# One compare for both one-hot tiles, their gates multiplied on ScalarE, and a norm's inverse root through logarithm and exponential

## The chip, the cores and the metric

The kernel runs on one core of one Trainium2 chip. The metric is the device time of one execution in microseconds. Three runs of the kernel before took 4728.34, 4738.8 and 4741.7 us; the median is 4738.8 us.

Five engines work side by side, each taking its own instructions strictly in order, and wait for one another by semaphores: TensorE (PE in the rows, with PEld for its weight loads) multiplies matrices, VectorE (DVE) and ScalarE (ACT) work on tiles element by element, GpSimd (POOL) does the same more slowly and issues the row gathers, SyncE (SP) issues most transfers. TensorE runs at one of two clock levels, 1.2 or 2.4 GHz; the profile gives the granted clock of a stretch as a share of the higher one.

## The reference

One inference step of a decoder with two layers, over 512 prompt tokens and 8 x 8 sample tokens, all in float32. In each layer one projection feeds three mixers (attention over a window, gated linear attention called GLA, pooling). Their results are gated, added, projected, and a layer norm follows; then comes a layer of 16384 one-neuron experts ("PEER"), and another layer norm. Two pieces matter here.

The GLA mixer ends in a norm per head:

```python
ob = ob * lax.rsqrt(jnp.mean(jnp.square(ob), -1, keepdims=True) + RMS_EPS) * gla_norm_g.astype(jnp.float32)
ob = (ob.astype(x.dtype) * jax.nn.silu(gb.reshape(Bx, T, B_HEADS, B_DV))).reshape(Bx, T, B_V)
```

The expert layer picks, for each token and each of 8 heads, 16 of 128 x 128 experts, and weighs them by a softmax:

```python
eidx = jnp.take_along_axis(cidx.reshape(...), ci, axis=-1)
g = jax.nn.softmax(cscore, axis=-1)
h = jax.nn.gelu(jnp.einsum('thkd,td->thk', u, xi, ...), approximate=False)
return jnp.einsum('thk,thkd->td', (g * h).astype(v.dtype), v)
```

So each token has 128 picked experts (8 heads x 16), each with a gate `g`.

## The kernel before

**Stages of a layer.** The tokens are cut into two groups. Group 0 (256 prompt tokens and the 64 sample tokens, 320 columns) goes through the mixers first (`_p1`: attention, the branch of it, GLA, GLA's norm and branch, pooling and its branch, the output projection and layer norm); then its expert scores are made (`_query`). Group 1 (256 prompt tokens) goes through the same `_p1` with a background: while it runs, the experts of group 0 are selected. Then group 1's scores are made, and the dense stage follows: all 128 rows of experts are multiplied for 384 tokens, while the remaining 192 tokens fetch their experts row by row (`uvr`, gathered by GpSimd and weighed on VectorE). In the trace the first layer's group 0 takes about 0 to 560 us and its scores to 700 us, group 1's mixers to 1160 us, its scores to 1250 us, the dense stage to 2400 us; the second layer repeats this from there on.

**The scatter of the gates (`_spread`, L941 to L972).** The dense stage needs, for each expert and token, the gate or zero. `_spread` makes it for four tokens at a time. A tile `oh` holds two one-hot tables for them: `oh[:, 1]`, with a row for each of a token's 128 picks and a one in the column of one half of the expert's number (one compare of 128 x 512 on VectorE, L951), and `oh[:, 0]`, the same for the other half, with the gate in place of the one. For that the count `n.act_mul` says how many of the four tokens are compared without a gate (L953) and multiplied by it on ScalarE (L958); the others take one VectorE instruction each that compares and multiplies (L960). TensorE multiplies the two tables of each token (L964), ScalarE copies the product into a staging tile `gst` (L965), and four transfers take each 32 tokens to memory (L971). Group 0's 256 tokens make 64 such fours in each layer, in the background of group 1's mixers, with `act_mul` 0; the last 128 tokens make 32 fours ahead of the dense stage, with `act_mul` 2 (L1171).

**The norm (`_phase_gla_out`, L567 to L601).** For each of four heads, GpSimd squares the two halves of the GLA output `oT`, TensorE sums them over the partitions with a matrix of ones (`ps_ssq`, L578), VectorE scales and adds the epsilon (L580), ScalarE takes the root in place (L583), and VectorE the reciprocal in place (L584). Each of the eight `oT` is then multiplied by that (L594) and by the gate of `gb` (L599). This is done four times: for each group of each layer, on 320 or 256 columns.

**The order.** Nobody writes the engines' order out. A scheduler places the instructions by priority and by its own reckoning of when each could start; the order on each engine is fixed when the program is built. The background of group 1's mixers is handed to it piece by piece, one or more at each fetch of a weight block (`tick`, L157), with a lower priority (`LAGB`). Weight blocks are cut on arrival into two parts for TensorE: ScalarE casts the high part (`whi`, L131), VectorE subtracts for the low part (`wlo`, L128), each with three buffers.

Of the kernel before, what the change touches and what calls it, by code (L numbers as in the profile page):

```python
# [15 lines left out]
AF = mybir.ActivationFunctionType  # L16
OP = mybir.AluOpType
# [549 lines left out]
def _phase_gla_out(n, l, oT):  # L567
    tc, nc, c, W = n.tc, n.nc, n.c, n.G.W
    ob = n.parts("ob")
    with tc.tile_pool(name="go_u", bufs=10) as up:  # L570
        n.up = up
        rs = []
        for h in range(4):
            ps = n.pmm.tile([128, 512], F32, tag="mm", name="ps_ssq", bufs=3)
            for dv in range(2):
                sq = n.unit("sq")
                nc.gpsimd.tensor_tensor(sq, oT[2 * h + dv], oT[2 * h + dv], op=OP.mult)
                nc.tensor.matmul(ps[:, 0:W], c["ones"], sq, start=(dv == 0), stop=(dv == 1))  # L578
            r = n.unit("rs")
            nc.vector.tensor_scalar(r, ps[:, 0:W], 1.0 / 256, RMS_EPS, op0=OP.mult, op1=OP.add)  # L580
            rs.append(r)
        for h in range(4):
            nc.scalar.activation(rs[h], rs[h], AF.Sqrt)  # L583
            nc.vector.reciprocal(rs[h], rs[h])  # L584
        for m in range(8):
            ps = n.mm(n.w_get(l, ("gb", m)), n.xs, W)
            b = BPOS["gb", m]
            th = n.unit("th")
            nc.scalar.activation(th, ps, AF.Tanh, scale=0.5, bias=n.hb[:, b:b + 1])
            xg = n.unit("xg")  # L590
            nc.scalar.activation(xg, ps, AF.Identity, bias=n.lc[:, b:b + 1])
            nc.vector.scalar_tensor_tensor(th, th, 1.0, xg, op0=OP.add, op1=OP.mult)
            o = oT[m]
            nc.vector.scalar_tensor_tensor(o, o, n.hg[:, m:m + 1], rs[m // 2], op0=OP.mult, op1=OP.mult)  # L594
            dst = [t[m // 4][:, m % 4, :] for t in ob]
            if len(dst) == 1:
                nc.vector.tensor_tensor(dst[0], o, th, op=OP.mult)
            else:
                nc.vector.tensor_tensor(o, o, th, op=OP.mult)  # L599
                n.put(dst, o)  # L600
    return [n.ks(t) for t in ob]  # L601
# [242 lines left out]
def _sel_tiles(sp, nt):  # L844
    return sp.tile([128, nt, 16, 16], F32, name="sv"), sp.tile([128, nt, 16, 16], U32, name="siu")
# [95 lines left out]
def _spread(n, gp, t, sT, new_ps, gt0=None):  # L941

    nc, c = n.nc, n.c
    iota = lambda w: c["iota"][:, None, None, :].to_broadcast([128, w, 4, 128])
    for g in range(128 // GT):
        st = gp.tile([128, 128, GT], F32, name="gst", bufs=n.gst)
        for t4 in range(0, GT, 4):
            tt = g * GT + t4
            oh = gp.tile([128, 2, 4, 128], F32, name="oh", bufs=n.job)
            w = n.act_mul  # L950
            nc.vector.tensor_tensor(oh[:, 1], iota(1)[:, 0], sT[:, 1, tt:tt + 4, None].to_broadcast([128, 4, 128]), op=OP.is_equal)  # L951
            if w:
                nc.vector.tensor_tensor(oh[:, 0, 0:w], iota(1)[:, 0, 0:w], sT[:, 0, tt:tt + w, None].to_broadcast([128, w, 128]),  # L953
                                        op=OP.is_equal)
            for k in range(4):
# [89 lines left out]
def tile_hybrid_step(ctx, tc, I, O, L):  # L1045
    nc = tc.nc
    n = Net(ctx, tc, I, O, L)
# [57 lines left out]
    for l in range(L):  # L1105
# [12 lines left out]
        gat.load(1, gpool)  # L1118
        sac, sa = scope(f"selA{l}")
        sv, siu = _sel_tiles(sa, 3)  # L1120
        n.job, n.gst, n.act_mul = 2, 1, 0
        _query(n, l, sa, [n.ks(xa[0]), n.ks(xa[1])], G0.tok, G0.W, sv, siu, n.new_mm)
        xac.close()
        sT = [sa.tile([128, 3, 128], F32, name=f"selT{t}") for t in range(2)]
# [40 lines left out]
        for q in range(2):  # L1165
            nc.gpsimd.tensor_tensor(x1W[q][:, :, 0:HB], x1A[0][q][:, :, 0:HB].bitcast(F32), x1A[1][q][:, :, 0:HB].bitcast(F32),
                                    op=OP.add)
# [40 lines left out]
        with tc.tile_pool(name=f"dense{l}", bufs=1) as dp:  # L1208
            gt, late = None, []
            for i in range(NE):  # L1210
# [12 lines left out]
                h = hs[i]  # L1223
# [206 lines left out]
```

## Time and profile before

| | |
|---|---|
| median of three runs | 4738.8 us |
| the profiled execution | 4736.97 us |
| its span, first to last instruction | 4735.2 us |
| mean granted clock of TensorE over the span | 0.978 |
| TensorE busy | 4530.7 us, 96% |
| VectorE busy | 3793.4 us, 80% |
| ScalarE busy | 1820.2 us, 38% |
| GpSimd busy | 1370.1 us, 29% |

A busy share over the whole span mixes stages with different limits, so the stage around the change has to be looked at by itself. Durations in the rows overlap a little where instructions follow each other without a wait: what one costs its engine in a row of equal ones is the step from start to start. A wait is given with the instruction that ended it.

### The profile page before, as it was taken

To read this page: it belongs to the slowest core of one execution; us is meant where nothing else is said; L and a number is where in the kernel's file an instruction comes from. 1 tells how busy PE (TensorE), PEld (TensorE's weight loads), DVE (VectorE), ACT (ScalarE), POOL (GpSimd) and SP (SyncE) were. 2 spreads that over 40 slices of the span, in tenths; PEclk is the share of its full clock that TensorE was granted. 3 is DMA by queue.
4 is the path that set the end of the run, shared out by engine and by line. 5 is a ranking of instruction groups with operands and counts; after the bars stand their busy time and mean duration, and the time that the engine had idled before them with its cause. 6 is when DMAs were issued, how large, how long until landed. Compare 5 with 4: busy or idle time off the path is not lost. (4 is left out here: it accounts for less than half of the span.)

```text
span 4735.2 us, 69451 instructions
## 1 busy us (share of the span) xinstructions
PE 4530.7 (96%) x25588; PEld 4001.3 (85%) x25588; DVE 3793.4 (80%) x7435; ACT 1820.2 (38%) x3386; POOL 1370.1 (29%) x884
## 2 busy tenths in 40 slices
PE   7999999989999999999999999999999999999998
PEld 6879977788778999999878789777887789999997
DVE  5455698697879999999964556977978799999998
ACT  3434323354343433333344343234433433333333
POOL 0011001121035555555300110011210365555552
PEclk9999999999999999999999999999999999999999
DMA  4334535566379899999723345265663798898996
GB/s 147 110 125 139 180 94 213 193 232 229 126 274 345 328 337 325 330 324 331 279 85 121 122 149 167 88 222 195 232 231 131 289 353 323 328 330 322 335 323 233
DMA packets 359521, 1093.59 MB, mean 231 GB/s; under 512 B 28495, under 2 KB 164175, under 8 KB 309709
## 3 DMA queue, kind: packets, MB, share of 16 engines
q1 hardware_dynamic: 272112, 608.88, 38.0%
q0 software_dynamic: 55296, 402.68, 22.6%
q10 hardware_dynamic: 31772, 77.60, 4.4%
q8 instruction: 201, 3.29, 0.3%
q14 instruction: 140, 1.14, 0.1%
HBM read 1014.01 MB, written 77.52 MB: 231 GB/s over the span
## 5 line engine op out<-in xcount | busy, mean ns | idle before, releaser
L128 POOL TENSOR_TENSOR wlo<-raw,whi 128x1024 fp32r<-128x1024 f32 x232 | 704.1, 3035 | 928.4 <-ACT whi L131 894.1
L131 ACT CAST whi<-raw 128x1024 fp32r<-128x1024 f32 x582 | 607.9, 1048 | 601.0 <-PE ps_mm L183 379.0
L183 PE MATMUL ps_h<-x1A,whi 128*128 128x384 f32 x3712 | 696.4, 340 | 13.3 <-ACT h L1182 13.2
L183 PEld LDWEIGHTS ps_h<-x1A,whi 128*128 128x128 f32 x3712 | 655.9, 190 | 33.6 <-ACT h L1182 17.1
L128 DVE TENSOR_TENSOR wlo<-raw,whi 128x1024 fp32r<-128x1024 f32 x350 | 432.8, 1241 | 275.2 <-ACT whi L131 136.8
L1024 DVE SCALAR_TENSOR_TENSOR zB<-uvr,hc,zB 128x1024 f32<-128x1024 f32 x380 | 587.2, 1545 | 4.7
L1006 POOL DMA_INDIRECT uvr<-uv,gidx x384 | 441.8, 1151 | 474.9 <-DVE zB L1024 209.0
L1017 DVE SCALAR_TENSOR_TENSOR uvr<-uvr,x1B 128x1024 f32<-128x1024 f32 x384 | 493.4, 1285 | 68.9 <-DMA uvr<-uv,gidx 68.6
L1236 PE MATMUL y<-vh,wh 128*128 128x512 f32 x1536 | 478.1, 393 | 0.6 <-ACT vh L131 0.6
L1236 PE MATMUL y<-vl,wh 128*128 128x512 f32 x1536 | 476.5, 391 | 0.0
L1236 PE MATMUL y<-vh,wl 128*128 128x512 f32 x1536 | 474.9, 390 | 0.3 <-DVE wl L128 0.3
L183 PE MATMUL ps_mm<-xa,whi 128*128 128x320 f32 x2400 | 413.3, 321 | 14.7 <-ACT xa L131 14.7
L1225 DVE TENSOR_TENSOR h<-h,gt 128x384 f32<-128x384 f32 x256 | 395.8, 1551 | 11.5 <-ACT h L1182 7.0
L183 PEld LDWEIGHTS ps_mm<-xa,whi 128*128 128x128 f32 x2400 | 370.7, 194 | 33.8 <-ACT xa L131 15.3
L183 PE MATMUL ps_h<-x1A,wlo 128*128 128x384 f32 x1856 | 362.7, 338 | 0.0
L1236 PEld LDWEIGHTS y<-vl,wh 128*128 128x128 f32 x1536 | 288.7, 188 | 64.2 <-DVE vl L128 0.2
L1236 PEld LDWEIGHTS y<-vh,wl 128*128 128x128 f32 x1536 | 288.7, 188 | 63.5 <-DVE wl L128 0.7
L131 ACT CAST wh<-h 128x384 fp32r<-128x384 f32 x256 | 130.5, 511 | 533.3 <-PE y L1236 502.0
L183 PEld LDWEIGHTS ps_h<-x1A,wlo 128*128 128x128 f32 x1856 | 327.1, 189 | 0.0
L1236 PEld LDWEIGHTS y<-vh,wh 128*128 128x128 f32 x1536 | 287.3, 189 | 45.7 <-ACT vh L131 1.4
L1019 ACT ACTIVATE hc<-hc 128x1 f32<-128x1 f32 x384 | 77.7, 203 | 628.1 <-DVE uvr L1017 620.3
L128 DVE TENSOR_TENSOR vl<-vr,vh 128x1024 fp32r<-128x1024 f32 x256 | 311.5, 1217 | 0.7 <-ACT vh L131 0.7
(349 smaller groups left out, 7650.3 us busy)
## 6 DMA issues: line engine op xcount, KB each, us to landing
raw<-wall SPq DMA_DIRECT2D x468, 512.0 KB
raw<-ut SPq DMA_DIRECT2D x256, 512.0 KB
vr<-vt SPq DMA_DIRECT2D x256, 512.0 KB
gd<-gst ACTq DMA_DIRECT2D x96, 512.0 KB
gt<-gd SPq DMA_DIRECT2D x62, 768.0 KB
S<-state_gla SPq DMA_DIRECT2D x8, 1024.0 KB
s_gla<-S ACTq DMA_DIRECT2D x8, 1024.0 KB
uvr<-uv,gidx POOLq DMA_INDIRECT x384
```

What stands on the lines that cost most here:

```text
L128: return eng.tensor_tensor(lo, src, hi.bitcast(F32), op=OP.subtract)
L131: return self.nc.scalar.copy(hi, src), self.sub_lo(lo, src, hi, eng)
L183: self.nc.tensor.matmul(ps[:, 0:W], w[wi][:, k * 128:(k + 1) * 128], xs[xi][k], start=(a == 0 and k == 0), stop=(a == len(pa) - 1 and k == ...
L1006: self.n.nc.gpsimd.indirect_dma_start(out=r, out_offset=None, in_=self.n.I["uv"], in_offset=bass.IndirectOffsetOnAxis(ap=self.idx[t][:, s: ...
L1017: nc.vector.scalar_tensor_tensor(r[:, 0:1024], r[:, 0:1024], 1.0, self.x[t], op0=OP.mult, op1=OP.mult, accum_out=hc[:, 0:1])
L1019: nc.scalar.activation(hc[:, 1:2], hc[:, 0:1], AF.Gelu)
L1024: nc.vector.scalar_tensor_tensor(acc, r[:, 1024:2048], hc[:, 1:2], acc, op0=OP.mult, op1=OP.add)
L1225: nc.vector.tensor_tensor(h3, h3, gt[:, :, i % 4, :], op=OP.mult)
L1236: nc.tensor.matmul(y[t][d], wt[:, ts], vt[:, d * 512:(d + 1) * 512], start=(j == 0 and a == 0), stop=(j == NE - 1 and a == 2))
```

## The change

The two compares of a four become one over both tables (1024 columns) where `act_mul` is 4, and `act_mul` becomes 4 for group 0's tokens; the gates of all four are then multiplied on ScalarE. The last 128 tokens (`act_mul` 2) take the same instructions as before. In the norm, the root and the reciprocal become a logarithm and an exponential of -0.5 times it, both on ScalarE, all four heads' logarithms written ahead of the exponentials.

```diff
         for h in range(4):
-            nc.scalar.activation(rs[h], rs[h], AF.Sqrt)
-            nc.vector.reciprocal(rs[h], rs[h])
+            nc.scalar.activation(rs[h], rs[h], AF.Ln)
+        for h in range(4):
+            nc.scalar.activation(rs[h], rs[h], AF.Exp, scale=-0.5)
...
             w = n.act_mul
-            nc.vector.tensor_tensor(oh[:, 1], iota(1)[:, 0], sT[:, 1, tt:tt + 4, None].to_broadcast([128, 4, 128]), op=OP.is_equal)
-            if w:
+            if w == 4:
+                nc.vector.tensor_tensor(oh, iota(2), sT[:, 0:2, tt:tt + 4, None].to_broadcast([128, 2, 4, 128]), op=OP.is_equal)
+            else:
+                nc.vector.tensor_tensor(oh[:, 1], iota(1)[:, 0], sT[:, 1, tt:tt + 4, None].to_broadcast([128, 4, 128]),
+                                        op=OP.is_equal)
                 nc.vector.tensor_tensor(oh[:, 0, 0:w], iota(1)[:, 0, 0:w], sT[:, 0, tt:tt + w, None].to_broadcast([128, w, 128]),
                                         op=OP.is_equal)
...
-        n.job, n.gst, n.act_mul = 2, 1, 0
+        n.job, n.gst, n.act_mul = 2, 1, 4
```

The scheduler then writes another order. In the program of the change VectorE has 128 compares of 128x1024 in place of 128 of 128x512 and 512 TENSOR_SCALAR, and 16 reciprocals fewer; ScalarE has 512 more multiplies by a gate, 16 more activations of `rs`, and 78 loads of an activation table where there were 74. The same instructions stand on TensorE, GpSimd and SyncE, some of them in another place. Lines after L583 have moved by one, those after L955 by four.

VectorE in group 1's pooling of the first layer (`u_ext`, `s_ext` and `d` belong to the pooling, `wlo` to the weights, `oh` to the scatter), before:

```order
L659 TENSOR_TENSOR s_ext<-u_ext 128x270
L951 TENSOR_TENSOR oh<-ct,selT_6264 128x512
L662 SCALAR_TENSOR_TENSOR d<-s_ext,u_ext 128x256
L960 TENSOR_SCALAR oh<-ct,selT_6264 128x128 x3
L128 TENSOR_TENSOR d_9369<-d,d_9368 128x256
L960 TENSOR_SCALAR oh<-ct,selT_6264 128x128
L128 TENSOR_TENSOR wlo<-raw,whi 128x1024
```

The same engine and place in the program of the change:

```order
L660 TENSOR_TENSOR s_ext<-u_ext 128x270
L953 TENSOR_TENSOR oh<-ct,selT_6264 128x1024
L663 SCALAR_TENSOR_TENSOR d<-s_ext,u_ext 128x256
L128 TENSOR_TENSOR wlo<-raw,whi 128x1024
L128 TENSOR_TENSOR d_9369<-d,d_9368 128x256
```

The four TENSOR_SCALAR are gone, and the weight's low part now stands ahead of that of `d`. ScalarE at this place, before:

```order
L131 CAST d_9368<-d 128x256
L131 CAST whi<-raw 128x1024
L652 ACTIVATE u_ext<-ps_mm,lc 128x256
L965 COPY gst<-ps_hr 128x128x4
L675 COPY oprow<-pt 15x128
```

and in the change:

```order
L131 CAST d_9368<-d 128x256
L653 ACTIVATE u_ext<-ps_mm,lc 128x256
L962 ACTIVATE oh<-oh,selT_6264 128x128
L969 COPY gst<-ps_hr 128x128x4
L676 COPY oprow<-pt 15x128
L962 ACTIVATE oh<-oh,selT_6264 128x128 x3
L131 CAST whi<-raw 128x1024
```

Multiplies by a gate now stand between the cast of one weight block and that of the next.

VectorE in group 0's last GLA head of the first layer, where the norm of the heads before it is already under way (`S` is the GLA state of that head, `klm` a masked key, `oT` the GLA output, `rs` the norm), before:

```order
L580 TENSOR_SCALAR rs<-ps_ssq 128x320
L506 TENSOR_TENSOR klm<-kl,ct 64x1024
L526 COPY S<-ps_S 128x256
L584 RECIPROCAL rs<-rs 128x320
L528 SCALAR_TENSOR_TENSOR S<-S,dec,ps_S 128x256
L584 RECIPROCAL rs<-rs 128x320
L528 SCALAR_TENSOR_TENSOR S<-S,dec,ps_S 128x256
L594 SCALAR_TENSOR_TENSOR oT_1732<-oT_1732,hg,rs 128x320
L528 SCALAR_TENSOR_TENSOR car_S_91<-S,dec,ps_S 128x256
```

The same place in the change:

```order
L580 TENSOR_SCALAR rs<-ps_ssq 128x320
L526 COPY S<-ps_S 128x256
L506 TENSOR_TENSOR klm<-kl,ct 64x1024
L528 SCALAR_TENSOR_TENSOR S<-S,dec,ps_S 128x256
L595 SCALAR_TENSOR_TENSOR oT_1732<-oT_1732,hg,rs 128x320
L528 SCALAR_TENSOR_TENSOR S<-S,dec,ps_S 128x256
L595 SCALAR_TENSOR_TENSOR oT_1733<-oT_1733,hg,rs 128x320
L528 SCALAR_TENSOR_TENSOR car_S_91<-S,dec,ps_S 128x256
```

The two reciprocals between the state's updates are gone, and two multiplies of `oT` stand there. ScalarE a little before, at the first head's norm, in the change (`os` is the sample tokens' GLA output, which TensorE takes next):

```order
L583 ACT_TABLE_LOAD
L583 ACTIVATE rs<-rs 128x320
L585 ACT_TABLE_LOAD
L585 ACTIVATE rs<-rs 128x320
L540 COPY os<-ps_os 64x256
```

Before, the third and fourth of these rows were not there: the copy of `os` followed the root of L583 at once.

## Rows read from the trace of the kernel before

**Rows 1.** The page's busy times: engine, us, share of the span, instructions

```profile
PE 4530.7 (96%) x25588; PEld 4001.3 (85%) x25588; DVE 3793.4 (80%) x7435; ACT 1820.2 (38%) x3386; POOL 1370.1 (29%) x884
```

**Rows 2.** Busy us of each engine in stretches, then granted clock, DMA share, GB/s

```profile
300.00:340.00 40.00, 36.77 (x174) 25.80 (x173) 25.67 (x42) 9.04 (x19) 6.35 (x8) 0.91 0.31 104
800.00:1160.00 360.00, 335.75 (x2377) 309.37 (x2375) 289.02 (x604) 164.51 (x288) 56.64 (x53) 0.97 0.58 204
1025.00:1150.00 125.00, 119.41 (x982) 117.01 (x982) 111.97 (x249) 64.35 (x109) 13.48 (x15) 0.99 0.57 192
1400.00:2325.00 925.00, 922.62 (x4663) 838.61 (x4662) 872.27 (x989) 357.74 (x609) 509.67 (x265) 1.00 0.91 331
2655.00:2700.00 45.00, 40.98 (x201) 29.72 (x200) 27.95 (x45) 10.34 (x21) 6.64 (x9) 0.92 0.37 123
3140.00:3515.00 375.00, 352.52 (x2459) 323.92 (x2457) 303.95 (x630) 166.53 (x293) 56.65 (x54) 0.97 0.59 207
```

**Rows 3.** TensorE's waits, 800 to 1160: ended by, us, times, longest

```profile
PE ps_hr L964 <- DVE oh L960: 6.1, 4, 3.9
...
PE ps_mm L183 <- DVE oc L633: 3.0, 1, 3.0
```

**Rows 4.** TensorE's waits, 3140 to 3515

```profile
PE ps_hr L964 <- DVE oh L960: 6.3, 5, 3.9
```

**Rows 5.** VectorE in order of time, 1050 to 1076: start, us, what

```profile
1055.32 1.11 DVE L960 TENSOR_SCALAR oh<-ct,selT 128x128 f32<-128x128 f32 x4
1056.35 0.69 DVE L951 TENSOR_TENSOR oh<-ct,selT 128x512 f32<-128x512 f32 x1
1056.95 1.11 DVE L960 TENSOR_SCALAR oh<-ct,selT 128x128 f32<-128x128 f32 x4
...
1072.69 2.36 DVE L128 TENSOR_TENSOR wlo<-raw,whi 128x1024 fp32r<-128x1024 f32 x2
```

**Rows 6.** ScalarE in order of time, 1255 to 1300

```profile
1281.81 1.28 ACT L958 ACTIVATE oh<-oh,selT 128x128 f32<-128x128 f32 x4 [2.65 <-DVE cv L812]
```

**Rows 7.** TensorE's waits over the span

```profile
PE ps_yr L964 <- ACT oh L958: 13.2, 12, 2.4
```

**Rows 8.** ScalarE's groups by form: xcount | busy us, mean ns | idle before

```profile
L449 ACT ACT_TABLE_LOAD x4 | 5.1, 1283 | 0.1
...
L583 ACT ACTIVATE rs<-rs 128x320 f32<-128x320 f32 x8 | 3.8, 471 | 11.3 <-DVE rs L580 11.3
```

**Rows 9.** All engines in order of time, 296 to 332

```profile
304.60 3.67 PE L538 MATMUL ps_os<-S,qm 128*64 128x256 f32 x16
...
309.56 0.43 PE L553 MATMUL ps_o<-ct,os 64*128 64x64 f32 x2 [0.24 <-ACT os L540]
...
320.36 2.13 DVE L584 RECIPROCAL rs<-rs 128x320 f32<-128x320 f32 x1
...
320.49 0.70 PE L523 MATMUL ps_S<-vb,kl 64*128 64x256 f32 x2 [0.75 <-DVE S L526]
...
322.72 2.13 DVE L584 RECIPROCAL rs<-rs 128x320 f32<-128x320 f32 x1
...
322.85 1.22 PE L523 MATMUL ps_S<-vb,kl 64*128 64x256 f32 x2 [1.30 <-DVE S L528]
...
325.63 5.29 PE L538 MATMUL ps_os<-S,qm 128*64 128x256 f32 x16 [0.95 <-DVE oT L594]
```

**Rows 10.** All engines in order of time, 926 to 962

```profile
934.48 2.08 PE L183 MATMUL ps_mm<-x,whi 128*128 128x256 f32 x16
...
958.25 0.77 PE L964 MATMUL ps_hr<-oh 128*128 128x128 f32 x2 [3.90 <-DVE oh L960]
...
958.66 2.91 PE L183 MATMUL ps_mm<-x,whi 128*128 128x256 f32 x12
```

**Rows 11.** Waits of all engines, 1000 to 1100

```profile
ACT whi L131 <- PE ps_mm L183: 21.3, 14, 3.3
```

**Rows 12.** VectorE's compares of L951 in 1025 to 1150: us, count

```profile
1025.00:1150.00 125.00, 22.31 (x30) 0.99 0.57 192
```

## The prediction

> **What bounds the kernel now.** I read the page's busy times first, then the stretches, then TensorE's waits in the stretches that the change touches, and last the order in time around the largest of those waits.
>
> The page has TensorE busy for 96% of the span, VectorE for 80% and ScalarE for 38% [rows 1]. The stretches say where these shares come from [rows 2]. In the dense stage (1400 to 2325 us, and the like of it in the second layer) TensorE is busy for 922.62 of 925 us at full clock: nothing that the change does reaches it, since that stage holds none of the changed instructions. The scatter of group 0's gates lies in group 1's mixers, 800 to 1160 us and 3140 to 3515 us. There TensorE is busy for 335.75 of 360 and 352.52 of 375 us, so that 24.2 and 22.5 us are left in which it does nothing; VectorE is busy for 289 and 304 us, ScalarE for 165 and 167. The norm of group 0 lies in 300 to 340 us, with 3.2 us of TensorE idle and a granted clock of 0.91. So the kernel is bound by TensorE, and all that the change can win is what TensorE now idles in these stretches, some 47 us in the scatter's two and 3 to 4 us in each of group 0's norms, and what it loses by a lower clock after idling. VectorE's own saving is worth only as much of it as it ends a wait of TensorE.
>
> Which waits are those? Of the scatter's two stretches, TensorE waited 6.1 and 6.3 us for the gated one-hots of L960, and twice 3.0 us for the pooling's output `oc`, which VectorE makes behind scatter work [rows 3, 4] (the row for `oc` reads the same in the second layer and stands once): 18.4 us in all. The rest of the idle time is made of smaller waits for VectorE, ScalarE and GpSimd.
>
> **The scatter: what VectorE saves.** Two fours in a row show the cost of one: from the four TENSOR_SCALAR at 1055.32 over the compare at 1056.35 to the next four at 1056.95 are 1.63 us [rows 5]. The compare of 128x1024 is not in the trace. Nearest is another float32 TENSOR_TENSOR of 128x1024, the low part of the weights: two of them take 2.36 us, so 1.18 each [rows 5]. From below, a compare of half the size takes 0.69 us [rows 5]; from above, two such take 1.38. I take 1.18. A four then costs VectorE 0.45 us less (0.94 to 0.25 by the bounds), and 128 fours 58 us, 29 in each layer (120 to 32 by the bounds). VectorE in 800 to 1160 falls from 289 to about 253 us, the norm's 7 us there included (below), 70% of the stretch in place of 80%.
>
> How much of that TensorE gets: the 18.4 us of waits above stand where VectorE has hardly a gap (1050 to 1075 us is mostly a row of instructions back to back, of which [rows 5] show some). With a quarter less scatter work in front of them I take three quarters of these waits as gone: -14 us. It may be none (the wait is then ended by something else a moment later) or all of it and some of the small ones, -25.
>
> After a long wait TensorE is also slower for a while: behind the wait of 3.90 us at 958.25, 12 matmuls took 2.91 us, where 16 of the same took 2.08 at 934.48, or 1.56 for 12 [rows 10]: 1.35 us more. There are four waits of 3.0 us or more among those of [rows 3, 4], two in each layer (3.9 and 3.0). If all go, 4 x 1.35, -5 us; if none, 0.
>
> **The scatter: what ScalarE pays.** Four multiplies by a gate in a row take it 1.28 us [rows 6]; 64 fours are 82 us in each layer. It had 165 of 360 us in work and will have about 247, 69%. Where fours stand densest, 1025 to 1150 us with 30 compares [rows 12], it goes from 64.35 to 103 of 125 us, 82% [rows 2]. It has room for this, but it stands on TensorE's path twice: the high part of every weight block is its cast, and a four's product now can't start before it has multiplied. Those are new waits. The nearest row is the last scatter (32 fours in each layer, two gates of four on ScalarE): TensorE waited 13.2 us for these multiplies over its 64 fours, 0.21 us each [rows 7]. By that the 128 fours of the first scatter would cost 26 us. But there the fours stand one behind the other, with little else for TensorE, while here they are spread among weight blocks of 3 us, with two buffers of `oh`. I take a fifth, +5 us, with 0 and 26 as ends. What lies behind a multiply that waits for its compare is, by the order shown, the cast of the next weight block; there are three buffers for these, so a delay of one four is covered, of two or three not.
>
> **The norm.** VectorE loses 16 reciprocals, 2.13 us each at 320 columns [rows 9]. In group 0 two of them stand between the updates of the GLA state, and TensorE waits for these: 0.75, 1.30 and 0.95 us at 320.49, 322.85 and 325.63 [rows 9]; the matmuls of `ps_os` behind the last then take 5.29 us, where the same sixteen took 3.67 at 304.60: 1.6 more. Sum 4.6 us in each layer. Against it stand a table load and an exponential ahead of the copy of `os`, which TensorE waited for at 309.56 [rows 9]: a load takes 1.28 us, an activation of `rs` 0.47 [rows 8], so +1.75. Net -2.9 in each layer, -6 us for both. If the state's updates wait for something else at once, only the +1.75 is left, +3.5; if the copy is not in time's way, -9. In group 1 the four reciprocals (about 1.7 us each) stand in VectorE's backlog ahead of the 3.90 us wait of [rows 10], and their going is part of the term above; the loads there fall into ScalarE's wait for the sums. If that cover is gone, the two loads and the exponentials ahead of the first gate of `gb` cost some 3 us in each layer, which three buffers of `ps_mm` take up.
>
> Each logarithm and exponential here comes with a load of its own in the program of the change, as the order shows, and the trace of before has it alike: the GLA gate's logarithm (L449) follows its exponential (L447) at once, and yet has loads of its own, 4 of 1283 ns [rows 8]. The Trainium skill (ScalarE: Activation LUTs, Table sets: the hidden batching unit) says that one set holds both, so that a logarithm and then an exponential need a single load. The trace does not agree for this program. By that rule the `os` copy would come 1.28 us earlier in each layer, and the sum would be 2.6 us lower.
>
> **The sum.** -14 (waits for VectorE) - 5 (clock) + 5 (waits for ScalarE) - 6 (norm) = -20 us. The profiled execution took 4736.97 us (span 4735.2 and 1.8 around it), so 4717 us. Its time stands 1.8 us below the median of the three runs, 4738.8, which differ by 13 us among themselves; I leave the forecast at 4717.
>
> **The rivals.**
>
> *The waits change hands.* VectorE is lighter, but TensorE then waits for ScalarE at the same places, because the four's chain (compare, multiply, product, copy) has become longer by 1.28 - 0.45 us. For it: ScalarE already spent 21.3 us of 1000 to 1100 us waiting for TensorE to free weight buffers [rows 11], in which nothing behind it moves. Against it: most of the order on TensorE stays, with the fours spread widely. The terms of the scatter then cancel (-14 - 5 + 19), only the norm is left: 4731 us.
>
> *ScalarE becomes late: slower.* Its place is the pooling and branch stretch of 1025 to 1150 us, where it would be at 82%, and in order. A multiply that waits for VectorE's compare holds the cast of the next weight block, that one TensorE; TensorE idles and drops to the lower clock, and the next four comes later still. At the last scatter's 0.21 us for each of 128 fours, and the waits for VectorE left as they are, it comes out at +26 - 6 = +20; at twice that, as four gates are on ScalarE here where two are there, at +53 - 6 = +47. I put it at 4757 us, the first of these. It decides from a cost of about 0.2 us a four, if VectorE's relief is worth nothing. The Trainium skill speaks for this one (ScalarE: Activation LUTs, Rules for kernel authors): multiplications belong on VectorE, not on ScalarE. The rows agree that a multiply is dearer there, as one four's gates take 1.28 us where VectorE compares and multiplies in 1.11.
>
> *More goes than the named waits.* The scheduler lays the lighter queue out closer, and half of the 47 us of idle time goes with the clock's losses after it: -24 - 11 (half of the 3% of clock that is missing in these 735 us [rows 2]) - 6 + 4 for new waits = -37, about 4700 us.
>
> **How the numbers follow.** 0.3% of this time, about what a measurement can tell from none, is 14 us; the bounds are 4725 and 4753. Chances: forecast 0.46 (its own range 4705 to 4728), more goes 0.13, the waits change hands 0.28, ScalarE late 0.13. Faster by over 0.3%: most of the first (0.40), all of the second, a little of the third: 0.55. Slower: 0.08 of the last. Within: 0.37. The range that leaves out no more than two in ten goes from 4696 to 4748: the lower end takes in the last rival, the upper end goes half of the way from no change to the slower one.
>
> **What would show it.** In 800 to 1160 us (or where these stages then lie) VectorE should be busy some 36 us less and ScalarE some 85 more; the waits of TensorE for `oh` from VectorE and for `oc` should be gone or under 2 us, and those for `oh` from ScalarE near 5 us over both layers. The compare should take 1.1 to 1.25 us. In group 0's norm the two stalls of 0.75 and 1.30 us should be gone, `ps_os` should take 3.7 us, and one of about 2 us for `os` should stand earlier. The dense stage should keep its length. The forecast is wrong if TensorE's idle time in the scatter's stretches is not smaller by 10 us or more; it is wrong the other way if casts of weights come late behind multiplies, with waits of TensorE on `wlo` or `whi`.

## The result, and the profile after

The changed kernel takes 4778.7 us (median of four runs, 4776.5 to 4785.3) where the kernel before takes 4737.8 beside it: ratio 1.0087, 95% interval 1.0074 to 1.0100, so 41 us slower. I had forecast 4717 us, and 4748 as the upper end. The profiled execution has a span of 4783.3 us, 48.1 more than that of before.

First the page's busy times of the changed kernel, which answer to [rows 1].

```profile
PE 4551.5 (95%) x25588; PEld 4012.3 (84%) x25588; DVE 3699.1 (77%) x6907; ACT 1983.9 (41%) x3918; POOL 1371.7 (29%) x884
```

VectorE is relieved by 94 us and ScalarE loaded with 164, as the change says. But TensorE, with the same 25588 matmuls, is busy 20.8 us longer (the mean granted clock is 0.975, before 0.978), and idle for 231.8 in place of 204.5 us (span less busy), 27.3 more. The two make up the 48.1.

Then the same stretches as in [rows 2]. The stages have shifted by up to 50 us, so these rows answer to those of before only roughly; group 1's pooling, before at 1025 to 1150, now lies at 1047 to 1172.

```profile
300.00:340.00 40.00, 35.42 (x140) 24.59 (x141) 17.01 (x32) 12.89 (x21) 4.84 (x6) 0.75 0.32 106
800.00:1160.00 360.00, 329.47 (x2245) 299.51 (x2246) 244.60 (x338) 224.54 (x526) 61.05 (x53) 0.96 0.57 196
1047.00:1172.00 125.00, 116.88 (x951) 113.91 (x951) 95.94 (x124) 94.86 (x224) 12.56 (x13) 0.99 0.56 189
3140.00:3515.00 375.00, 337.85 (x2183) 300.06 (x2182) 254.62 (x415) 215.94 (x506) 59.37 (x61) 0.95 0.57 200
```

VectorE fell to 245 us of 360 (I had said 253), yet TensorE's idle time rose from 24.2 to 30.5 us there, and from 22.5 to 37.2 in the second layer. Group 0's norm ran at a granted clock of 0.75, before at 0.91.

For a sum by stage I took, in each trace, the ends of the last matmuls of `ps_lr` (after attention), `ps_ssq` (after GLA and norm) and `ps_wo` (after the output). Lengths in us, one profile each, so a single difference of a few us says little. Group 0's GLA and norm are the exception, since many kernels below share them: with the norm of before they read 140.5 to 147.7 (22 readings, median 141.9), with the changed norm 145.5 to 148.7 (12 readings, median 148.2).

```
                        before  changed  norm alone  scatter alone
group 0 GLA+norm, 1st    142.0    148.2       148.0          144.7
group 0 GLA+norm, 2nd    141.9    145.5       148.7          147.7
group 1 to ps_lr, 1st    244.5    245.7       246.9          249.5
group 1 GLA+norm, 1st    122.8    128.8       123.3          126.0
group 1 to ps_wo, 1st    229.2    232.6       225.4          228.6
group 1 to ps_lr, 2nd    243.2    248.1       243.9          244.2
group 1 GLA+norm, 2nd    122.9    132.6       117.1          131.2
group 1 to ps_wo, 2nd    226.7    235.5       226.3          226.6
```

What TensorE waited for over the span of the changed kernel (us, times, longest):

```profile
PE ps_hr L968 <- ACT oh L962: 25.8, 25, 3.1
...
PE ps_mm L183 <- DVE th L240: 16.5, 2, 8.3
...
PE ps_os L538 <- DMA S<-state_gla: 5.6, 3, 3.0
...
PE ps_mm L183 <- DVE oc L634: 4.8, 6, 1.4
...
PE ps_o L553 <- ACT os L540: 3.8, 2, 2.0
```

The waits for `oh` from VectorE of [rows 3, 4] are gone, those for `oc` smaller. In their place stand four others. My sum had those for `oh` from ScalarE, at a fifth of this, and for `os`, at about this length (3.5 us); those for `th` and for the state it did not have. Three places show how they come about.

**Group 0's norm.** The changed kernel in order of time; behind the table loads stands the copy of `os`:

```profile
309.69 1.28 ACT L583 ACT_TABLE_LOAD   x1
...
311.48 1.28 ACT L585 ACT_TABLE_LOAD   x1
...
313.15 0.35 ACT L540 COPY os<-ps_os 64x256 f32<-64x256 f32 x1
...
313.55 0.69 PE L553 MATMUL ps_o<-ct,os 64*128 64x64 f32 x2 [2.02 <-ACT os L540]
...
319.70 3.72 PE L560 MATMUL ps_S<-vb,klm 64*128 64x256 f32 x8
...
325.52 0.38 ACTq L564 DMA_DIRECT2D s_gla<-S  x1
...
330.03 0.38 SPq L472 DMA_DIRECT2D S<-state_gla  x1
...
335.31 6.11 PE L538 MATMUL ps_os<-S,qm 128*64 128x256 f32 x16 [2.36 <-DMA S<-state_gla]
```

And three rows of the kernel before that my prediction had not read:

```profile
312.93 1.94 PE L560 MATMUL ps_S<-vb,klm 64*128 64x256 f32 x8
...
315.81 0.38 ACTq L564 DMA_DIRECT2D s_gla<-S  x1
...
320.33 0.38 SPq L472 DMA_DIRECT2D S<-state_gla  x1
```

The copy came 1.8 us later against its matmuls, as worked out. But TensorE, idle for 2.02 us, then ran at the lower of its two levels (eight matmuls 3.72 us for 1.94; 1.2 GHz for 2.4), so the state's updates ended late, its store was issued at 325.52 for 315.81, and the next state's load, which waits for the store since `S0` has one buffer, at 330.03 for 320.33. In the kernel before `ps_os` began at 325.63 [rows 9], 5.3 us after that load was issued; here 335.31, again 5.3 us after. So the load was due when the reciprocals' stalls ended; a kernel below (e5) shows it without them.

**The end of group 1's GLA.** TensorE runs out of weight blocks and waits for a gate's multiply, which stands behind a table load and two exponentials of GLA:

```profile
920.62 1.28 ACT L481 ACT_TABLE_LOAD   x1
...
923.01 0.40 ACT L962 ACTIVATE oh<-oh,selT 128x128 f32<-128x128 f32 x1
...
923.46 1.40 PE L968 MATMUL ps_hr<-oh 128*128 128x128 f32 x4 [2.47 <-ACT oh L962]
```

Behind both places TensorE is slow for longer than the wait: the granted clock of the changed kernel (third number from the end) is 0.55 and 0.72 in these stretches; in before it is 0.87 and 0.92 where they answer to (311 to 326, 901 to 931).

```profile
313.00:328.00 15.00, 14.45 (x44) 10.67 (x45) 5.46 (x13) 3.74 (x8) 1.44 (x2) 0.55 0.11 36
920.00:950.00 30.00, 24.68 (x106) 19.44 (x105) 18.20 (x21) 17.47 (x39) 12.02 (x11) 0.72 0.26 91
```

**Group 1's branches.** VectorE's row stands still at a gathered row that has not landed. Behind it is `th`, where VectorE takes a product out of PSUM (L240) and so frees the buffer that TensorE waits for. In the trace by engine:

```profile
1004.90 1.70 POOL L1010 DMA_INDIRECT uvr<-uv,gidx  x1 [6.45 <-DVE zB L1028]
...
1014.42 1.22 DVE L1021 SCALAR_TENSOR_TENSOR uvr<-uvr,x1B 128x1024 f32<-128x1024 f32 x1 [6.33 <-DMA uvr<-uv,gidx]
...
1015.57 0.41 DVE L240 SCALAR_TENSOR_TENSOR th<-th,ps_mm 128x256 f32<-128x256 f32 x1
...
1016.04 3.72 PE L183 MATMUL ps_mm<-x,whi 128*128 128x256 f32 x16 [8.27 <-DVE th L240]
```

The waits for `oh` from ScalarE lie in more than one place. Of 11.8 us in the first layer 4.1 are in GLA and up to the norm's first load, 3.1 just behind the norm's loads, 4.6 in the pooling stretch. The longest in each layer (2.70 and 3.15 us) has a transfer behind it: ScalarE's multiplies stand behind copies into `gst`, its one staging buffer, whose last transfer has not ended.

```profile
1150.34 1.07 ACT L969 COPY gst<-ps_hr 128x512 f32<-128x512 f32 x2 [2.04 <-DMA gd<-gst]
...
1151.77 1.67 PE L968 MATMUL ps_hr<-oh 128*128 128x128 f32 x8 [2.70 <-ACT oh L962]
```

### The profile page after: what moved, and what is told of

Read it like the earlier page. It is cut to its first block, busy times and chain, and to the rows that moved or that the text cites. A ratio compares the mean times of both kernels' runs of the same rounds, so it can differ in the third digit from the quotient of the medians.

```text
span 4783.3 us, 69483 instructions
## 1 busy us (share of the span) xinstructions
PE 4551.5 (95%) x25588; PEld 4012.3 (84%) x25588; DVE 3699.1 (77%) x6907; ACT 1983.9 (41%) x3918; POOL 1371.7 (29%) x884
## 3 DMA queue, kind: packets, MB, share of 16 engines
q0 software_dynamic: 55296, 402.68, 22.5%
## 4 chain that ended last, share of the span: by engine, by line
PE 79%; DVE 7%; DMA 6%; ACT 3%; issue 3%; POOL 1%; ACTq 0%; SPq 0%; DVEq 0%; POOLq 0%
PE ps_mm L183 21%; PE ps_h L183 20%; PE y L1240 20%; PE ps_yr L183 2%; PE ps_v L464 2%; PE ps_wo L755 2%; PE ps_hr L968 2%; DMA uvr<-uv,gidx 2%; DMA gd<-gst 2%; DMA raw<-wall 1%; PE ps_o L553 1%; PE po L357 1%; PE ps_sc L826 1%; PE ps_S L560 1%; PE ps_S L523 1%
## 5 line engine op out<-in xcount | busy, mean ns | idle before, releaser
L1021 DVE SCALAR_TENSOR_TENSOR uvr<-uvr,x1B 128x1024 f32<-128x1024 f32 x384 | 484.6, 1263 | 85.0 <-DMA uvr<-uv,gidx 84.3
```

What stands on the lines that cost most here:

```text
L1021: nc.vector.scalar_tensor_tensor(r[:, 0:1024], r[:, 0:1024], 1.0, self.x[t], op0=OP.mult, op1=OP.mult, accum_out=hc[:, 0:1])
```

## The experiments

Medians are given with the ratio to the kernel before that ran beside; that kernel's own medians were 4739.0 (e1 to e4), 4738.5 (e5 to e8), 4739.9 (e9 to e12), 4735.7 (e13 to e16), 4744.8 (e17) and 4732.8 (e18). Where two versions did not run side by side, a difference of their medians is uncertain by some of this spread.

**The two parts alone.** `e1_norm_only` is before with the lines of Ln and Exp; `e2_onehot_only` is the change with Sqrt and reciprocal put back.

> The norm's logarithm and exponential alone, with the scatter as it was. Theory (a late copy): in group 0's norm the copy of os comes some 1.8 us later, TensorE waits 2 us for it and runs at the lower clock for some 12 us behind, so that the last update of the GLA state, its store and the load of the next state come late; TensorE then waits for that load. In the trace of the changed kernel the stretch lost 7.5 us in the first layer and 3.6 in the second: this kernel takes about 11 us more than before, 4745 to 4753. Rival (my forecast's step): the reciprocals' going is worth more than the late copy, -6 us, 4731. Second rival: the norm is lost in the scatter's effects, no change (within 4 us).

Measured 4753.1, ratio 1.0032 [1.0016, 1.0047]: +14, at the upper end of the theory's range.

> The merged compare with the gates multiplied on ScalarE alone, with the root and the reciprocal as they were. Theory: the remaining 30 of the 41 us come from here, TensorE's waits for the gated one-hots from ScalarE (26 us in the changed kernel) and for a gather that VectorE's row waits for (8 us in each layer): 4763 to 4773. Rival: the scatter is worth little by itself and the two parts harm each other (ScalarE late because of both): 4740 to 4750, and the two parts alone add to less than half of 41 us.

Measured 4761.4, ratio 1.0039 [1.0021, 1.0056] (median +22): just under the range given, and far over the rival's. The two together make 36 of the 41 us. The table by stage shows the norm losing 6 to 7 us in each layer in group 0, and winning some 6 in all in group 1.

**Gates on VectorE, on GpSimd, on ScalarE by half.**

```
e3  + nc.vector.tensor_tensor(oh[:, 0], oh[:, 0], <gates of the four>, op=OP.mult)
e9  + nc.gpsimd.tensor_tensor(oh[:, 0], oh[:, 0], <gates of the four>, op=OP.mult)
e11   before, with act_mul = 2
```

> As the one before, but the four gates are multiplied on VectorE, in one instruction of 128x512 behind the merged compare; ScalarE has no part in the one-hots. A four costs VectorE 1.2 + 0.7 = 1.9 us, 0.3 more than before. Theory (the chain through ScalarE costs): the waits for oh from ScalarE are gone, those for oh from VectorE are as before or somewhat longer, 4736 to 4752. Rival (any change of the order costs as much, the merge itself included): 4760 or more.

4752.2, ratio 1.0031 [1.0014, 1.0049]: at the upper end of the theory's range, with 18.0 us of waits for `oh` from VectorE. It reads 9 us less than e2, but the two intervals overlap. And its GLA and norm in group 1 took 135.2 and 133.5 us, longer than e2's 126.0 and 131.2: a loss there needs no multiply on ScalarE.

> The merged compare with the old norm, and the gates multiplied on GpSimd, in one instruction of 128x512 for a four. GpSimd was busy for 29% of the span. Theory (what costs is that a four's product comes late behind a third, in-order engine, whichever it is): TensorE waits for oh from GpSimd instead, 15 us or more in all, 4750 or more. Rival (it is ScalarE's own queue, its table loads and casts, that makes the multiply late): with a nearly idle engine the waits for oh fall under 8 us in all, and the time goes to that of before or below, 4715 to 4740.

4814.4, ratio 1.0154 [1.0137, 1.0171]. The waits on GpSimd in this kernel:

```profile
PE ps_hr L970 <- POOL oh L953: 30.9, 21, 5.8
```

An engine that is idle for most of the span is no better place. The multiply of 128x512 took 1534 ns there (128 of them), 699 on VectorE in e3. The Trainium skill (GPSIMD Engine Reference, Engine selection) puts two-input elementwise work on VectorE, GpSimd being some two times slower; these rows agree, 2.2 times.

> Before, with two of four gates multiplied on ScalarE in group 0's scatter (a compare of 512 and one of 256, two multiplies on ScalarE, two fused on VectorE). Theory (the wait for ScalarE's multiplies is what costs): about half of the cost of four, 4744 to 4756. Rival (the cost comes from elsewhere and VectorE's relief is worth something): 4740 or less.

4756.3, ratio 1.0031 [1.0019, 1.0044]: +16, more than half; TensorE's wait for ScalarE's multiplies was 30.1 us, no less than with four gates. The cost does not show in proportion to the multiplies, and e12 below costs 10 with none of them moved.

**Group 0's norm taken apart.**

```
e4  changed:   - nc.scalar.copy(os, ...)   + nc.vector.tensor_copy(os, ...)
e5  e1:        + with tc.issue_after(<last copy of os>):  around Ln and Exp in group 0
e6  e5:        - S0 bufs=1                 + S0 bufs=2
e10 before:    Ln and Exp in group 1 alone
```

> The changed kernel with one more edit: the copy of os out of PSUM is made by VectorE, not by ScalarE, so that it no longer stands behind the table loads and exponentials of the norm. Theory (a late copy): the wait of TensorE of 2.0 us for os in group 0's norm goes, with the low clock and the late load of the state behind it; 8 to 11 us less than the changed kernel, 4768 to 4771. Rival (the late load of the state comes from somewhere else, as the store is issued by ScalarE behind its loads): less than 4 us gained, 4775 or more.

4782.9, ratio 1.0097 [1.0064, 1.0129]: nothing won, so the expectation failed. The trace says why: on VectorE the copy stands behind a multiply that waits for `rs`, and so for the same loads.

```profile
311.27 0.41 DVE L540 COPY os<-ps_os 64x256 f32<-64x256 f32 x1
...
311.74 0.43 PE L553 MATMUL ps_o<-ct,os 64*128 64x64 f32 x2 [3.14 <-DVE os L540]
```

> The norm's logarithm and exponential alone (the scatter as before), and in group 0 queued on ScalarE behind the last copy of os, so that no table load stands ahead of that copy; the moving of the copy to VectorE had not removed the wait but made it 3.1 us. Theory (a late copy lowers the clock, and the state's load ends the stall in any case): the first os wait and the low clock behind it are gone, so that group 0's GLA and norm take 142 us again in each layer (148 with the norm's change alone); but TensorE now waits some 2.5 to 3 us for the load of the next state in place of the 0.75, 1.30 and 0.95 us for VectorE, so nothing is won there. Group 1's 3 to 6 us a layer remain: 4728 to 4737 in all. Rival (my forecast's step): with the copy out of the way the reciprocals' 4.6 us of each layer are won as well: group 0's stage 137 us, 4715 to 4724.

4751.2, ratio 1.0023 [1.0011, 1.0034]. Neither in full: the wait for `os` is gone, and the store and the load of the state stand where they stood before (315.62, 320.12), but TensorE, early now, waits longer for that load than expected and drops to the lower level behind it; the stage took 146.8 and 147.2 us.

```profile
326.58 6.54 PE L538 MATMUL ps_os<-S,qm 128*64 128x256 f32 x16 [4.59 <-DMA S<-state_gla]
...
333.59 1.28 ACT L586 ACT_TABLE_LOAD   x1
...
336.43 0.71 PE L553 MATMUL ps_o<-attT,vb 128*128 128x128 f32 x4 [1.18 <-ACT oT L554]
```

That wait is less than half of the loss, though: `ps_os` ended 2.0 and 2.5 us later in the stage than in the kernel before, the stage 4.8 and 5.3. e18 below has such a wait too, and its stage took 141.4 and 141.6 us. From the end of `ps_os` to the end of the stage, however, it is 10.8 and 10.9 us here, 8.1 before and 7.4 in e18: the norm's loads, now behind the last copy of `os`, stand ahead of a copy of `oT` (L554) for which TensorE waits, and it drops to the lower level again (the eight matmuls of L560 took 3.00 us, 1.94 in e18).

> As the one before, with a second buffer for the state S0, so that the load of the next head's state need not wait until this head's is stored. Theory (the state's load is what ends last): TensorE's wait for the state is gone, group 0's stage is 3 to 4 us shorter than in the one before in each layer, 6 to 8 us in all. Rival (the load is late for another reason, the transfers beside it, or the GLA's chain is as long by itself): within 3 us of the one before.

4750.2, ratio 1.0021 [1.0009, 1.0032]. The stage took 142.5 us in both layers, 4.3 and 4.7 less, as the theory said, and the wait for the state is gone. It is no shorter than before all the same: there is a new wait for GpSimd's squares, and behind `ps_os` it takes 10.8 and 10.6 us as in e5. The medians are only 1 us apart, though: the stages behind it, to `ps_wo`, read 230.5 and 229.1 us here (224.4 and 225.9 before), and I can't say why.

```profile
317.69 2.19 PE L578 MATMUL ps_ssq<-sq,ct 128*128 128x320 f32 x4 [2.16 <-POOL sq L577]
...
327.03 3.67 PE L538 MATMUL ps_os<-S,qm 128*64 128x256 f32 x16
```

> The logarithm and the exponential in group 1's norm alone; group 0's norm has its root and reciprocal, the scatter is as before. Theory (the change of the norm gains in group 1, where the reciprocals stand in VectorE's backlog, and loses in group 0): group 0's GLA and norm take 142 us in both layers, group 1's stages keep the 6 us (both layers together) that they gained with the norm's change alone: 4730 to 4735. Rival (the gain was a chance of one profile, or the wait for the gathered row gives it back): 4738 or more.

4733.8, ratio 0.9989 [0.9976, 1.0001]: -6, as expected, though the interval just takes in no change; group 0's stage took 141.7 and 141.9. From here to e1, which differ by group 0's norm alone, it is 19 us by the medians and 12.4 by the two profiles.

**The scatter's buffers and the gathered rows.**

```
e7  changed:  n.job = 3 (buffers of oh);  pool_u bufs=3 -> 2
e8  changed:  EARLY = 26 -> 0
e16 e10:      EARLY = 26 -> 20
```

> The changed kernel with three buffers of oh in place of two for group 0's scatter, paid for with two buffers in place of three for the units of pooling. Theory (two buffers are too few for a four's chain that has become 0.8 us longer and crosses an engine more): TensorE's waits for oh from ScalarE fall from 25.8 to under 13 us, and the time by 8 to 15 us, to 4764 to 4771. Rival (ScalarE comes late because it works in order, however many buffers there are): the waits stay over 20 us, 4775 or more.

4782.6, ratio 1.0090 [1.0065, 1.0114]. The waits for `oh` fell as the theory said, and the time stayed as the rival said:

```profile
PE pt L499 <- POOL ekl L495: 15.2, 9, 4.4
...
PE ps_hr L968 <- ACT oh L962: 10.8, 9, 2.1
...
PE ps_ssq L578 <- POOL sq L577: 5.4, 6, 1.8
PE ps_hr L968 <- ACT gst L969: 5.3, 4, 2.5
PE ps_mm L183 <- ACT xg L592: 5.3, 4, 2.3
```

The 15 us changed hands: TensorE was idle for 233.4 us in all, 231.8 in the changed kernel. The pooling's lost buffer does not explain it: group 1's branches, which hold the pooling, took 234.2 and 234.5 us, 232.6 and 235.5 in the changed kernel. The sum of waits under one name is therefore no measure of what they cost.

> The changed kernel with none of the 26 gathered rows weighed during group 1's mixers; the dense stage has to weigh them. Theory (VectorE's row stands still at the product of a gathered row that has not landed, and th of L240 behind it): TensorE's waits for th from VectorE, 16.5 us, fall under 2, and group 1's branches and output are 8 us or more shorter in each layer (232.6 and 235.5 in the changed kernel); the dense stage may take some of it back, as VectorE is busy there for 92% and gets 26 times some 3.4 us more. Rival (th is late because of VectorE's or ScalarE's load as such): the wait goes over to another tile and these stages stay within 4 us of those of the changed kernel.

4835.6, ratio 1.0197 [1.0171, 1.0222]. No wait for `th` from VectorE is left among the forty largest; group 1's branches took 223.2 and 221.4 us, 9.4 and 14.1 less, so the early gathered rows were the cause. The run takes away their work on VectorE along with the standing; that it is the standing is read from the 6.33 us of L1021 above, not shown by itself. The stages that hold the dense work grew by 51.8 and 50.7.

> A candidate: the norm's logarithm and exponential in group 1 alone (4733.8), with 20 in place of 26 gathered rows weighed during group 1's mixers. Theory (VectorE stands still at a gathered row there, with th behind it: 4.8 and 5.4 us of TensorE's waits in the kernel with 26): these waits fall under half, and the time to 4720 to 4730. Rival (the dense stage gives it back, as without any early rows it took 52 us more in each layer): 4736 or more.

4731.4, ratio 0.9984 [0.9975, 0.9993] over eleven runs. With six early rows fewer the wait is gone and the branches took 218.0 and 217.4 us (225.6 and 226.0 in e10), of which the dense stages took most back (+8.8 and +5.5). The time is above the 4720 to 4730 that I expected, but this is the one version whose interval lies below before's time. It isn't apart from e10, whose interval overlaps, though 10.2 us of waits for `th` are gone.

**The order.** e12 and e13 are before with the background's priority `LAGB` at -40 and -60 in place of -50; e14 and e15 the scatter's change alone with these; e17 the whole change at -60; e18 is e17 with the exponentials of a norm queued behind its last logarithm.

> A control: nothing of the work is changed, the priority of the background of group 1's mixers alone (-40 in place of -50), so that the scheduler lays the same instructions out a little differently. Theory (the costs found are those of the changed instructions): within 6 us of before, 4733 to 4745. Rival (the order before is a fine optimum, and nearly any other order costs some 10 us): 4748 or more.

4749.9, ratio 1.0020 [1.0011, 1.0030]: the rival is right. The same work in another order costs 10 us; in this one TensorE waits 17.5 us for `gst`.

> The second control: the work of before, the background's priority at -60 in place of -50. With -40 it took 4749.9, 10 more than before, with nothing of the work changed. Theory (the change of the scatter costs by its own chain, on top of a spread by order of some 10 us): 4739 to 4750. Rival (before's order is a single good one, and every other costs as much as the change of the scatter): 4755 or more.

4750.2, ratio 1.0030 [1.0019, 1.0040]: +15, just over the theory's end.

> The scatter's change alone, with the background's priority at -40. Theory (the chain through ScalarE costs in any order): 8 to 25 us more than the control with the same priority (4749.9), 4758 to 4775. Rival (what was measured at -50 was an unlucky order): within 6 us of that control or below it, 4756 or less.

4773.9, ratio 1.0090 [1.0069, 1.0110]: 24 over its control e12, which ran at another time (28 if each is set against the kernel before beside it).

> The scatter's change alone, with the background's priority at -60. Theory (the chain through ScalarE costs in any order): 8 to 25 us more than the control with -60 that runs beside it. Rival (an unlucky order at -50): within 6 us of that control or below it.

4751.2, ratio 1.0038 [1.0020, 1.0056]: 0.9 over its control e13, though TensorE's waits for `oh` from ScalarE add up to 27.0 us here too. So in three orders the scatter's change reads 22, 24 and 1 us.

> The whole change, with the background's priority at -60. There the scatter's change alone cost 0.9 us against its control, where it cost 22 to 24 at -50 and -40. Theory (the norm's 14 us are in group 0's stage, which lies before any background, and hold in any order; the scatter's cost hangs on the order): 4750 + 14 + 1, 4760 to 4770. Rival (the two parts together make ScalarE late in any order): 4775 or more, 25 over the control with -60 (4750.2).

4791.2, ratio 1.0105 [1.0080, 1.0130]: 41 over the control e13 (32 if each is set against the kernel before beside it); the rival's figure is right. In this order group 1's norm came in three parts, each with its two loads, with gates in between, and the fourth product of `gb` (the gate of GLA's output) waits for `xg`, which frees its PSUM buffer, behind it all. ScalarE, first and last of a row of six loads, and TensorE behind it:

```profile
941.12 1.28 ACT L583 ACT_TABLE_LOAD   x1
...
952.13 1.28 ACT L585 ACT_TABLE_LOAD   x1
...
955.34 0.46 ACT L592 ACTIVATE xg<-ps_mm,lc 128x256 f32<-128x256 f32 x1
...
955.86 2.18 PE L183 MATMUL ps_mm<-x,whi 128*128 128x256 f32 x16 [1.93 <-ACT xg L592]
```

TensorE's waits over the span:

```profile
PE ps_mm L183 <- ACT xg L592: 25.8, 8, 9.1
PE ps_hr L968 <- ACT oh L962: 25.3, 19, 4.6
```

Of the 25.8 us the row of loads has little. Two of the eight waits, 9.11 us and in the second layer 8.15, make 17.3, and they stand some 27 us later: VectorE stands at a gathered row, ScalarE's cast of `ob` waits for what VectorE has behind that, and `xg` stands behind the cast.

```profile
979.86 1.22 DVE L1021 SCALAR_TENSOR_TENSOR uvr<-uvr,x1B 128x1024 f32<-128x1024 f32 x1 [5.69 <-DMA uvr<-uv,gidx]
...
981.92 0.41 ACT L131 CAST ob<-oT 128x256 fp32r<-128x256 f32 x1 [9.66 <-DVE oT L600]
...
983.24 1.86 PE L183 MATMUL ps_mm<-x,whi 128*128 128x256 f32 x7 [9.11 <-ACT xg L592]
```

> The kernel before this one (the whole change at -60, 4791.2), with the exponentials of a norm queued on ScalarE behind its last logarithm, so that each of the four norms loads two tables; there the heads came one by one and group 1's norm loaded six, 12.9 us of ScalarE from the first load to the last exponential with three gates in between, while TensorE waited 25.8 us in all for xg behind it. Theory (ScalarE's queue in group 1's norm, loads and multiplies together, is where the two parts harm each other): the waits for xg fall under 10 us and group 1's branches (243.8 and 243.4) are shorter by 6 us or more in each layer: 4765 to 4778. Rival (the multiplies alone make ScalarE late, the loads only show it): waits for xg or for other tiles of ScalarE stay, 4785 or more.

4774.1, ratio 1.0085 [1.0058, 1.0112]: 17 less by the medians, though the intervals overlap, and not mostly from where I said. Group 0's stages gave it: 141.4 and 141.6 us for 148.3 twice, since only one load now stands ahead of the first copy of `os`, as before the change. That settles group 0's loss: it is the second load and the exponential in that place. The wait for the state is there all the same (3.56 and 3.63 us), so without the late copy the reciprocals' going wins next to nothing. Group 1's branches gave 3.8 and 3.7 us. The waits for `xg` fell to 17.5, not under 10: the 1.93 us behind the loads is gone in both layers, the waits behind a gathered row stayed (7.95 and 7.87).

```profile
326.32 6.41 PE L538 MATMUL ps_os<-S,qm 128*64 128x256 f32 x16 [3.56 <-DMA S<-state_gla]
```

```profile
PE ps_hr L969 <- ACT oh L963: 22.2, 18, 3.5
PE ps_mm L183 <- ACT xg L593: 17.5, 4, 8.0
```

## Why the prediction was wrong

Two terms of the sum had the wrong sign, one came out at its upper end, and in one the waits went but the time did not. For group 0's norm the cause is shown (e1, e10, e18). For the scatter TensorE's new waits, and the lower clock behind them, stand in the trace; that they make its 22 us is argued, not shown.

- *The norm, -6 us: wrong, +14 (e1).* The step that failed is "Sum 4.6 us in each layer", with "Net -2.9". The three stalls of [rows 9] were counted as winnable, although the state's load came in when they ended. Without them TensorE waits for the load (4.59 us in e5, 3.56 in e18), and in e18, where the copy is not late either, the stage took 141.4 and 141.6 us for 142.0 and 141.9: won 0.6 and 0.3 us, not 4.6. My bound "if the state's updates wait for something else at once, only the +1.75 is left, +3.5" named this case, but took the delay of the copy at its bare length. It brought TensorE to the lower level, and through the store and the load it came back as 6 to 7 us in each layer (e1, e18). In group 1, where I had put the reciprocals under VectorE's waits, about 6 us seem won in all (e10, whose interval just takes in none).
- *The clock, -5 us: wrong sign.* "If all go, 4 x 1.35, -5 us; if none, 0": I priced only the waits that go, and no new ones. TensorE was busy 20.8 us longer (clock 0.975 for 0.978).
- *Waits for ScalarE, +5 us with 26 as the upper end: mis-sized.* They are 25.8 us, 0.20 for each of 128 fours, which is the rate of the last scatter [rows 7] without the fifth that I took of it. But the runs do not let me call that sum the price: with 10.8 (e7) the time was the same, and with 27.0 (e15) the change cost next to nothing.
- *Waits for VectorE, -14 us: they went, the time didn't come.* `oh` fell from 12.4 to nothing, `oc` from 7.5 to 4.8. Waits for `th` behind gathered rows rose from 0.6 to 16.5; e1 has 9.1 of it, e2 hardly any, but with the old norm e3 has 6.5 and e9 15.8, so it is not the norm's alone. e8 shows that the early rows make it. I had not asked what VectorE meets next when it gets through its row sooner: a transfer.
- *VectorE's cost of a four: right.* The merged compare took 1.27 us in the mean of the 64 in 800 to 1200 us (I took 1.18, bounds 0.69 to 1.38), the four gates 1.27 us in a row.
- *The rivals.* "ScalarE becomes late: slower" (0.13) has the sign, and the multiply that is late stands in the trace; that it makes the time is not shown (e3, e7, e15). Its place was right in part only: the pooling, now at 1047 to 1172, has 4.6 of the first layer's 11.8 us of these waits and 8.1 us of idle time, 5.6 before [rows 2], at a clock of 0.99. The rest is in GLA and behind the norm's loads in group 1, where the same queue has table loads. The Trainium skill's rule that I set beside it (ScalarE: Activation LUTs, Rules for kernel authors: multiplications on VectorE) spoke for the side that came out; e3, with them on VectorE, reads 9 us less than e2, within the intervals. By its rule on loads (Table sets: the hidden batching unit) each Ln and Exp pair would have needed one; the changed kernel has 10 of L583 and 10 of L585, of 1283 ns each.

What stays open: how much of the scatter's cost is its chain and how much the order. Before's order is better than its two neighbours by 10 and 15 us, so up to that much of the 22 may be the loss of a good order; the change of the scatter was 1, 22 or 24 us above the same work in the same setting.

## What to carry to other kernels

A stall on the bounding engine is worth its length only if nothing else arrives as it ends: read what the next wait would be, transfers above all, before counting it as won. When work goes to a lighter engine, look not at its share but at what stands in its queue just behind and ahead of the moved instructions, in the few places where the bounding engine has no other work: there a wait of 2 us cost 6 to 7 here. Follow a wait past the engine that is named: those for `xg` from ScalarE in e17 were mostly VectorE's, at a transfer. And where a scheduler makes the order, run the same work in a second and third order before a difference of a few tenths of a per cent is put down to the change.

## What the runs showed of the hardware

Behind a wait of 2.02 us TensorE ran at its lower level for most of the next 15 us (granted clock 0.55 from 313 to 328); I had priced waits of 3 us and more, at 1.35 us each. The same instructions in the same order (group 0's GLA and norm, of before) took 140.5 to 147.7 us in different profiles. That may be part of why this kernel's executions differ by 30 us (4721.1 to 4751.6 beside e1 to e4); no run shows it.
